# A chunked scan whose operands are laid out by head of a pair in DRAM, with a tied store and a reordered output projection

## The chip, the cores and the metric

One core of a Trainium2 chip runs the whole program. The metric is the device time of one execution in microseconds (us). Engines are named as in the profile: PE (TensorE, its weight loads apart as PEld), DVE (VectorE), ACT (ScalarE), POOL (GpSimd) and SP (SyncE), which here only issues DMAs; its queue is called SPq. Every engine and every queue works its instructions off in the order in which they stand there.

## The reference

Two layers over 1024 tokens of width 1024. Layer 0 is a convolution and gating mixer, layer 1 an RWKV-7 time mixing; after each mixer and after each SwiGLU feed-forward part stands `x <- LN(alpha*x + ...)`. The change touches layer 1's time mixing:

```
r, k, v = projections of shifted x;  decay w, gate g, rate a from low-rank projections
kk = normalized k * k_k;  k = k * (1 + (a - 1) * k_a)          # 16 heads of 64
state = state * w + (state @ -kk) * (kk * a) + v * k           # per token, per head
y_t   = state @ r_t
y = group norm(y) * ln_g + ln_b + sum(r * k * r_k) * v;   mix = (y * g) @ w_out
```

## The kernel before, in words

`build` calls the phases in order: `phase_a` (layer 0's mixer), `ffn` 0, `phase_c` (the projections of layer 1), the scan `phase_d`, `phase_e` (the output projection of the scan's y) and `ffn` 1. Large matmuls are written as three products of fp32r halves (`mm3`, L232 to L234), weights arrive through three raw buffers (tag `wraw`, `raw_load`, L177) and are split by ACT and DVE (`load_unit`, L192 and L193).

**Phase C** computes R, K, KN, KA, SW (decay) channel-major and spills each tile of 128 channels x 512 tokens with one DMA (`spill`, L836) into DRAM tensors `[8 chunks of 128 tokens, 128, 8, 128]`, where the third index is the pair of heads. V is computed token-major and spilled by `do_v` with one DMA per 128 tokens x 512 columns (L1044) into a plain `[1024, 1024]` tensor `scr_v`.

**The scan** has 32 units: 16 chunks of 64 tokens by two groups of four head pairs. One unit holds, on 128 partitions, two heads of a pair in the two halves of the partitions, called e = 0 and 1. A unit's inputs come by 13 DMAs: `load` (L1209) issues SW and KN (L1219), K and KA in four half-partition DMAs (L1223) and R (L1225); `load_v` (L1228) issues UV and V by halves (L1235, L1236). Its result y leaves by two half-partition DMAs (`store`, L1446) into `scr_y`, plain `[1024, 1024]`.

The units are software-pipelined by hand. Step i of the main loop emits first `store` of unit i-1, then `load` of unit i+5 and `load_v` of unit i+2, then interleaves generators by the letters of `ORDER` (L77): E is `cumulate` of unit i+4 (it reads SW on DVE at L1242, and ACT follows at L1248), D `decay` of unit i+3, P `scores` of unit i+2, I `inverse` of unit i+1, C the eight parts of `chain` of unit i. The sixth C holds the state update (pS) and the last two C's the group norm and gate of y: after PE and DVE, y passes through a chain of POOL instructions (L1415 to L1431), the last of which is the multiplication by the gate at L1431. A scheduler orders the instructions of each queue by the program's order and its own model of when inputs and buffers are ready; `pace` ties an instruction behind the last matmul in that schedule without a semaphore. Buffers of the scan come from rings (`rings`, L1177): y has two, V three.

**Phase E** works on tiles of 128 tokens, tt = 0 to 7. `get_y(tt)` loads the 128 x 1024 tile of y with one DMA (through a `wraw` buffer) and the residual `xres` (L1518), applies gain and bias to the residual on POOL (`ln_gain`, L355 and L356), and transposes y on PE (L1525). `mmh(tt, n)` makes half n of the output columns, 24 matmuls. `ln(tt)` normalizes (the power on POOL is L272, the normalized tile ACT L279) and transposes the result on PE (L298). Two tiles' first halves run inside the scan's last steps (`early`). After the scan the order is: the four units of `w_out`'s second half are loaded; tiles 2 and 3 are fetched and their first half made; tiles 4 to 7 are fetched in a row; then the second halves of tiles 0 to 3 with their `ln`; then the second halves of tiles 4 to 7; then their first halves with `ln`.

Of the kernel before, what the change touches and what calls it, by code (L numbers as in the profile page):

```python
# [15 lines left out]
F32 = mybir.dt.float32  # L16
# [9 lines left out]
P = 128  # L26
D = 1024
# [44 lines left out]
HP = 4  # L72
# [1 line left out]
AHEAD = 4  # L74
INV = 1

ORDER = "ICIPCEIPDICPIECDICPICICPDICI"  # L77
SCAN_EARLY = 32


# [9 lines left out]
def build(tc, xT, xtok, w_ab, w_abv, w_abo, cols, rows, hrows, sguw, f_in, f_out, w_r, w_k, w_v, w_o,  # L90
          l_w1, l_a1, l_g1, l_w2, l_a2, l_g2, out, dbg=None):
    nc = tc.nc
    c = Ctx()
    c.tc, c.nc = tc, nc
    c.first_loads = None
    with ExitStack() as es:
        setup(c, es, rows, hrows)
        dram = es.enter_context(tc.tile_pool(name="dram", bufs=1, space=DRAM))
        xres = dram.tile([T, D], F32, name="xres")
        scr = {n: dram.tile([8, P, 8, P], F32, name=f"scr_{n}") for n in ("R", "K", "KN", "KA", "SW")}  # L100
        scrv = dram.tile([T, D], F32, name="scr_v")
        scry = dram.tile([T, D], F32, name="scr_y")

        def show(n, tiles):
            if dbg is not None and n in dbg:
                for i, a in enumerate(tiles):
                    nc.sync.dma_start(dbg[n][i * P:(i + 1) * P, :], a)
        res = [dram.tile([T, D], F32, name=f"res{i}") for i in range(2)]
        hscr = dram.tile([NHT, P, T], F32, name="scr_h")
        xc = phase_a(c, xT, xtok, w_ab, w_abv, w_abo, sguw, cols, res[0])  # L110
        def masks():
            c.scan = scan_const(c)
        x1 = ffn(c, 0, xc, f_in, f_out, "mix0", "ffn0", res[0], hscr, fp32_out=True, spill=xres, aside=masks)
        if dbg is not None and "b" in dbg:
            nc.sync.dma_start(dbg["b"], xres)
        scan = phase_d(c, scr, scrv, scry, l_g2)
        phase_c(c, x1, scr, scrv, w_r, w_k, w_v, l_w1, l_a1, l_g1, l_w2, l_a2, scan)
        if dbg is not None and "R" in dbg:
            for n in scr:
                nc.sync.dma_start(dbg[n], scr[n])  # L120
            nc.sync.dma_start(dbg["V"], scrv)
        xc = phase_e(c, scry, xres, w_o, scan, res[1])
        if dbg is not None and "Y" in dbg:
            nc.sync.dma_start(dbg["Y"], scry)
        ffn(c, 1, xc, f_in, f_out, "mix1", "ffn1", res[1], hscr, final=out)


# [26 lines left out]
def tmp(c, name, dtype=F32):  # L154
    return c.pool.tile([P, 512], dtype, name=name, tag="t", bufs=N_T)
# [673 lines left out]
def phase_c(c, x1, scr, scrv, w_r, w_k, w_v, l_w1, l_a1, l_g1, l_w2, l_a2, scan):  # L829
# [2 lines left out]
    ghid = c.ghid = big(c, "ghid")  # L832

    def spill(n, k, h, src):
        dst = scr[n][4 * h:4 * h + 4, :, k, :].rearrange("c p t -> p c t")
        nc.sync.dma_start(dst, src.rearrange("p (c t) -> p c t", c=4))  # L836

    c.omu = c.const.tile([P, 48], F32, name="omu")
    nc.vector.tensor_scalar(c.omu, c.colr("mu", 0, 48), -1.0, 1.0, op0=ALU.mult, op1=ALU.add)
# [195 lines left out]
    def do_v(h, xi, rest=None, turn=None):  # L1035
        for n in range(2):
            units = [load_unit(c, w_v[n, q]) for q in range(4)]
            for t in range(4):
                p = bank(c, "a", "pv")
                proj_tok(c, p, units, xi, t, turn)  # L1040
                v = sp()
                nc.scalar.copy(v, p)
                tt = h * 4 + t
                nc.sync.dma_start(scrv[tt * P:(tt + 1) * P, n * 512:(n + 1) * 512], v)  # L1044
                if rest and n == t == 0:
                    rest()
                step(7 - n * 4 - t)
# [100 lines left out]
def phase_d(c, scr, scrv, scry, l_g2):  # L1148
# [21 lines left out]
    def rings(plan, n, dtype=F32):  # L1170
        pool, at = Ring(c, plan[0][0], n, sum(k for _, k in plan), dtype).bufs, 0
        for name, k in plan:
# [2 lines left out]
            at += k  # L1175
            R1[name] = r
    rings([("ra", INV + 3), ("bk", 2), ("bktm", NA), ("UV", INV + 3), ("AT", 2 * NA)], 2 * W)  # L1177
    rings([("R", 3), ("cl", 2), ("Em", 2), ("rk", 2), ("S", 2 * NG), ("dS", 2), ("u1", 2), ("y", 2),
           ("V", 3), ("gg", 2), ("bo", 2)], W)
    rings([("E", 4)], HP * (CH + 2))  # L1180
    rings([("TT", 2)], HP * P, F32R)
    rings([("zr", 3)], W, F32R)
# [26 lines left out]
    def load(n, ch, g):  # L1209
        u = Ctx()  # L1210
        u.n, u.ch, u.g = n, ch, g
        ks = slice(g * HP, (g + 1) * HP)
        at = slice(ch % 2 * CH, ch % 2 * CH + CH)
        src = lambda nm, r=slice(0, P): scr[nm][ch // 2, r, ks, at]
        u.ld = {}
        t_ = tmp(c, "ld")
        for e, nm in enumerate(("SW", "KN")):
            u.ld[nm] = A4(t_[:, e * W:(e + 1) * W])
            nc.sync.dma_start(u.ld[nm], src(nm))  # L1219
        u.xk = tmp(c, "ld").rearrange("p (k x t) -> p k x t", k=HP, x=2)  # L1220
        for e in range(2):
            for x, nm in ((e, "K"), (1 - e, "KA")):
                nc.sync.dma_start(u.xk[half[e], :, x, :], src(nm, half[e]))  # L1223
        u.ld["R"] = A4(R1["R"]())
        nc.sync.dma_start(u.ld["R"], src("R"))  # L1225
        us[n] = u

    def load_v(u):  # L1228

        src = scrv[u.ch * CH:(u.ch + 1) * CH, u.g * 2 * W:(u.g + 1) * 2 * W].rearrange(  # L1230
            "t (k e j) -> t e k j", k=HP, e=2)
        u.UV = R1["UV"]().rearrange("p (e k j) -> p e k j", e=2, k=HP)
        u.V = A4(R1["V"]())
        for e in range(2):
            nc.sync.dma_start(u.UV[half[e], e], src[:, e])  # L1235
            nc.sync.dma_start(u.V[half[e]], src[:, e])  # L1236

    def cumulate(u):

# [200 lines left out]
            pass  # L1440

    def store(u):
        dst = scry[u.ch * CH:(u.ch + 1) * CH, u.g * 2 * W:(u.g + 1) * 2 * W].rearrange(
            "t (k e j) -> t e k j", k=HP, e=2)
        for e in range(2):
            nc.sync.dma_start(dst[:, e], u.y[half[e]])  # L1446

    def by_half(name):

# [11 lines left out]
    through(decay(us[0]))  # L1461
    for i in range(-INV - 1, len(seq)):
        gens = {}
        if i > 0:
            store(us[i - 1])
        if i + AHEAD + 1 < len(seq):
            load(i + AHEAD + 1, *seq[i + AHEAD + 1])
        if 0 <= i + INV + 1 < len(seq):
            load_v(us[i + INV + 1])
        if i + AHEAD < len(seq):  # L1470
            gens["E"] = cumulate(us[i + AHEAD])
        if i + INV + 2 < len(seq):
            gens["D"] = decay(us[i + INV + 2])
        if i >= 0:
            gens["C"] = chain(us[i], us.get(i + NG))
        if 0 <= i + INV < len(seq):
            gens["I"] = inverse(us[i + INV])
        if i + INV + 1 < len(seq):
            gens["P"] = scores(us[i + INV + 1])
        if i == 0:  # L1480
            g2 = c.pool.tile([P, 1024], F32, name="g2", tag="w", bufs=N_W)
            nc.sync.dma_start(g2, l_g2)
            g2 = g2.rearrange("p (g k e j) -> p g e k j", g=NG, k=HP, e=2)
            lg, lb = by_half("rln_g"), by_half("rln_b")
        for s in ORDER:
            if s in gens:
                fresh[0] = True
                next(gens[s], None)
                if s in "CIP":
                    yield  # L1490
        for gen in gens.values():
            assert next(gen, "end") == "end"
    store(us[len(seq) - 1])

# [1 line left out]
def phase_e(c, scry, xres, w_o, scan, res):  # L1498
# [12 lines left out]
        return r  # L1511

    def get_y(tt, b):
        y = raw_load(c, scry[tt * P:(tt + 1) * P, :])
        yh = big(c, "yh", F32R).rearrange("p (k t) -> p k t", k=KT)
        yl = big(c, "yl", F32R).rearrange("p (k t) -> p k t", k=KT)
        acc[tt] = big(c, "acc")
        nc.sync.dma_start(acc[tt], xres[tt * P:(tt + 1) * P, :])  # L1518
        ln_gain(c, acc[tt], rows_)
        st[tt] = norm_stats(c, D)  # L1520
        for q in range(2):
            pt = bank(c, b, "pt", [P, 4, P])
            for j in range(4):
                k = q * 4 + j
                c.last_mm = nc.tensor.transpose(pt[:, j, :], y[:, k * P:(k + 1) * P], c.ident)  # L1525
            split(c, yh[:, q * 4:q * 4 + 4, :], yl[:, q * 4:q * 4 + 4, :], pt)
            yield
        ys[tt] = yh, yl
# [39 lines left out]
    assert next(scan, "end") == "end"  # L1568
    through(first)
    units[0][3] = load_unit(c, w_o[0, 3])  # L1570
    units[1] = [load_unit(c, w_o[1, q], arena=True) for q in range(4)]
    done = E_EARLY
    for h in range(2):
        for tt in range(4 * h, 4 * h + 4):
            if ys[tt] is None:
                through(get_y(tt, "b"))
            if tt >= done:
                through(mmh(tt, h, "a"))
        if h == 0:
            for tt in range(4, 8):  # L1580
                through(get_y(tt, "b"))
        for tt in range(4 * h, 4 * h + 4):
            through(mmh(tt, 1 - h, "a"))
            if tt % 4 >= E_LN:
                ln(tt - E_LN)
        for tt in range(4 * h + 4 - E_LN, 4 * h + 4):
            ln(tt)
    return xc


# [77 lines left out]
```

## Time and profile before

| what | value |
|---|---|
| median of 3 runs | 2655.47 us (2653.22 to 2659.98) |
| the profiled execution's own time | 2657.45 us |
| its span | 2655.7 us |
| mean granted PE clock | 0.971 of full |
| PE / PEld / DVE / ACT / POOL busy | 95% / 75% / 64% / 43% / 19% |
| first and last store of the scan's y | 1411.2 and 1858.5 us from the span's start |

A span is cut by the profile into 40 equal slices of 66.4 us. A busy PE is not PE at its peak, since matmuls overlap; idle time is shown with what ended it ("<-"). A wait is put down to the instruction that came last.

### The profile page before, as it was taken

To read this page: it belongs to the slowest core of one execution; us is meant where nothing else is said; L and a number is where in the kernel's file an instruction comes from. 1 tells how busy PE (TensorE), PEld (TensorE's weight loads), DVE (VectorE), ACT (ScalarE), POOL (GpSimd) and SP (SyncE) were. 2 spreads that over 40 slices of the span, in tenths; PEclk is the share of its full clock that TensorE was granted. 3 is DMA by queue.
4 is the path that set the end of the run, shared out by engine and by line. 5 is a ranking of instruction groups with operands and counts; after the bars stand their busy time and mean duration, and the time that the engine had idled before them with its cause. 6 is when DMAs were issued, how large, how long until landed. Compare 5 with 4: busy or idle time off the path is not lost.

```text
span 2655.7 us, 41419 instructions
## 1 busy us (share of the span) xinstructions
PE 2517.7 (95%) x16064; PEld 2004.7 (75%) x16064; DVE 1697.4 (64%) x2981; ACT 1136.5 (43%) x2192; POOL 517.8 (19%) x526
## 2 busy tenths in 40 slices
PE   8999999999999999999998878788899999999997
PEld 6677868888878786777777767676677888878785
DVE  7775596666648428777846667675477666657534
ACT  3115552323323327777746666674352333322230
POOL 0012250000007000010214555465300000006003
PEclk9999999999999999999998789899899999999999
DMA  3403322222235433555764333322223222225451
GB/s 145 125 20 109 115 84 88 87 80 80 81 126 198 150 124 107 163 157 165 207 164 101 91 89 86 76 52 96 105 88 103 80 87 74 86 99 188 146 169 64
DMA packets 257605, 295.79 MB, mean 111 GB/s; under 512 B 149888, under 2 KB 190976, under 8 KB 257408
## 3 DMA queue, kind: packets, MB, share of 16 engines
q1 hardware_dynamic: 256256, 291.05, 35.3%
q8 instruction: 126, 2.06, 0.3%
q10 hardware_dynamic: 1152, 2.10, 0.2%
q14 instruction: 71, 0.58, 0.1%
HBM read 219.56 MB, written 69.21 MB: 109 GB/s over the span
## 4 chain that ended last, share of the span: by engine, by line
PE 65%; DVE 9%; issue 9%; DMA 7%; POOL 6%; ACT 4%; SPq 1%; DVEq 0%; ACTq 0%; POOLq 0%
PE py L646 14%; PE pz L646 9%; PE px L646 8%; DMA wraw<-in_f_out_dram 2%; PE pv L232 2%; PE pd L232 1%; PE pd L233 1%; PE pd L234 1%; PE po L232 1%; PE po L233 1%; PE po L234 1%; PE pv L233 1%; POOL acc L355 1%; PE pv L234 1%; PE pA L1204 1%
## 5 line engine op out<-in xcount | busy, mean ns | idle before, releaser
L646 PE MATMUL py<-xch,wb 128*128 128x512 f32 x1056 | 356.5, 400 | 2.9 <-DVE u L695 2.1
L200 ACT CAST wb<-wraw 128x512 fp32r<-128x512 f32 x220 | 135.6, 619 | 398.6 <-PE py L646 177.4
L232 PE MATMUL pd<-wb,hh 128*128 128x512 f32 x704 | 277.5, 394 | 5.1 <-DVE acc L735 5.0
L234 PE MATMUL pd<-wb,hl 128*128 128x512 f32 x704 | 278.0, 395 | 0.0
L233 PE MATMUL pd<-wb,hh 128*128 128x512 f32 x704 | 277.7, 394 | 0.0
L646 PEld LDWEIGHTS py<-xch,wb 128*128 128x128 f32 x1056 | 199.7, 189 | 61.4 <-DVE u L695 15.3
L203 DVE TENSOR_TENSOR wb<-wraw,wb 128x512 fp32r<-128x512 f32 x220 | 171.8, 784 | 112.9 <-ACT wb L200 110.6
L355 POOL TENSOR_TENSOR acc<-acc,g_row 128x1024 f32<-128x1024 f32 x24 | 65.8, 2743 | 897.6 <-DMA acc<-res 880.3
L646 PE MATMUL px<-xch,wb 128*128 128x512 f32 x704 | 234.4, 396 | 3.3 <-ACT p L657 3.3
L646 PE MATMUL pz<-xch,wb 128*128 128x512 f32 x704 | 233.1, 392 | 4.5 <-ACT xch L200 4.5
L200 ACT CAST wb<-sums 128x512 fp32r<-128x512 f32 x176 | 108.8, 622 | 256.7 <-PE pz L646 145.2
L646 PE MATMUL py<-xcl,wb 128*128 128x512 f32 x528 | 209.0, 396 | 1.6 <-DVE xcl L203 1.6
L203 DVE TENSOR_TENSOR wb<-sums,wb 128x512 fp32r<-128x512 f32 x176 | 123.0, 702 | 102.6 <-ACT wb L200 101.7
L203 DVE TENSOR_TENSOR hl<-wraw,hh 128x1024 fp32r<-128x1024 f32 x72 | 126.9, 1771 | 89.5 <-ACT hh L200 89.4
L1204 PEld LDWEIGHTS <-lt 128*128 128x128 f16 x1792 | 88.0, 102 | 103.2 <-issue 77.7
L232 PEld LDWEIGHTS pd<-wb,hh 128*128 128x128 f32 x704 | 133.1, 189 | 37.3 <-issue 4.4
L646 PEld LDWEIGHTS px<-xch,wb 128*128 128x128 f32 x704 | 132.7, 189 | 35.2 <-ACT p L657 5.5
L646 PEld LDWEIGHTS pz<-xch,wb 128*128 128x128 f32 x704 | 132.0, 188 | 35.0 <-ACT xch L200 5.3
L1204 PE MATMUL pX<-lt 128*128 128x64 f16 x1280 | 92.2, 201 | 69.2 <-DVE lt L1337 38.8
L233 PEld LDWEIGHTS pd<-wb,hh 128*128 128x128 f32 x704 | 132.7, 189 | 30.0
L234 PEld LDWEIGHTS pd<-wb,hl 128*128 128x128 f32 x704 | 132.7, 189 | 29.7
L193 DVE TENSOR_TENSOR wlo<-wraw,whi 128x1024 fp32r<-128x1024 f32 x82 | 103.0, 1262 | 69.9 <-ACT whi L192 46.8
(313 smaller groups left out, 5706.6 us busy)
## 6 DMA issues: line engine op xcount, KB each, us to landing
wraw<-in_f_in_dram SPq DMA_DIRECT2D x96, 512.0 KB, 3.6
wraw<-scr_h SPq DMA_DIRECT2D x72, 512.0 KB, 3.9
scr_h<-hf SPq DMA_DIRECT2D x44, 512.0 KB, 2.6
wraw<-in_f_out_dram SPq DMA_DIRECT2D x88, 256.0 KB, 2.7
res<-acc SPq DMA_DIRECT2D x16, 512.0 KB, 2.6
acc<-res SPq DMA_DIRECT2D x16, 512.0 KB, 4.2
wraw<-in_w_r_dram SPq DMA_DIRECT2D x16, 512.0 KB, 4.0
wraw<-in_w_k_dram SPq DMA_DIRECT2D x16, 512.0 KB, 4.2
```

The lines of the kernel that those rows point to most:

```text
L193: (lo_eng or nc.vector).tensor_tensor(lo, raw, f(hi), op=ALU.subtract)
L200: nc.scalar.copy(hi, src)
L203: return (eng or nc.vector).tensor_tensor(lo, src, f(hi), op=ALU.subtract)
L232: nc.tensor.matmul(ps, ls(ah), rs(bh), start=start, stop=False)
L233: nc.tensor.matmul(ps, ls(ah), rs(bl), start=False, stop=False)
L234: c.last_mm = nc.tensor.matmul(ps, ls(al), rs(bh), start=False, stop=stop)
L355: c.nc.gpsimd.tensor_tensor(x, x, rows[0], op=ALU.mult)
L646: c.last_mm = nc.tensor.matmul(ps, a_[:, k * P:(k + 1) * P], b_[:, k % 2, :], start=start and k == i == 0, stop=False, skip_group_check=True)
L1204: keep(nc.tensor.matmul(*a, **k))
```

## The change

The DRAM tensors get layouts by head: K and KA together as `KB` with the two places that the scan's tile wants side by side, V and y as `[16 chunks, 2 (e), 64 tokens, 8 pairs, 64]`. A unit is loaded by 7 DMAs (SW, KN, KB, R, UV twice, V) and stored by one. The spills of K and KA in phase C take two DMAs each for one, those of V four for one; `get_y` takes four DMAs for one. `store` becomes a generator at a new letter Y in `ORDER`, behind the fifth C of the following step, tied by `pace` behind the last matmul there. The y ring grows from two to three buffers, V's from three to four; the number of arena tiles stays. In phase E tiles 2 and 3 are fetched and multiplied first, with the second half's weights loaded between; then second halves of tiles 0 to 3 with `get_y` of tiles 4 to 7 and `ln` between them; then first halves of tiles 4 to 7, then their second halves with `ln`.

```diff
-ORDER = "ICIPCEIPDICPIECDICPICICPDICI"
+ORDER = "ICIPCEIPDICPIECDICPIYCICPDICI"
...
-        scr = {n: dram.tile([8, P, 8, P], F32, name=f"scr_{n}") for n in ("R", "K", "KN", "KA", "SW")}
-        scrv = dram.tile([T, D], F32, name="scr_v")
-        scry = dram.tile([T, D], F32, name="scr_y")
+        scr = {n: dram.tile([8, P, 8, w, P], F32, name=f"scr_{n}") for n, w in (("R", 1), ("SW", 1), ("KN", 1), ("KB", 2))}
+        scrv, scry = [dram.tile([T // CH, 2, CH, 8, 64], F32, name=f"scr_{n}") for n in "vy"]
...
     def spill(n, k, h, src):
-        dst = scr[n][4 * h:4 * h + 4, :, k, :].rearrange("c p t -> p c t")
-        nc.sync.dma_start(dst, src.rearrange("p (c t) -> p c t", c=4))
+        name, places = dict(K=("KB", (0, 1)), KA=("KB", (1, 0))).get(n, (n, (0,)))
+        m = P // len(places)
+        for e, x in enumerate(places):
+            r = slice(e * m, (e + 1) * m)
+            dst = scr[name][4 * h:4 * h + 4, r, k, x, :].rearrange("c p t -> p c t")
+            nc.sync.dma_start(dst, src[r].rearrange("p (c t) -> p c t", c=4))
...
-                nc.sync.dma_start(scrv[tt * P:(tt + 1) * P, n * 512:(n + 1) * 512], v)
+                v5 = v.rearrange("p (k e j) -> p e k j", k=4, e=2)
+                for i in range(4):
+                    r = slice(i // 2 * CH, i // 2 * CH + CH)
+                    nc.sync.dma_start(scrv[2 * tt + i // 2, i % 2, :, n * 4:n * 4 + 4, :], v5[r, i % 2])
...
-    rings([("R", 3), ("cl", 2), ("Em", 2), ("rk", 2), ("S", 2 * NG), ("dS", 2), ("u1", 2), ("y", 2),
-           ("V", 3), ("gg", 2), ("bo", 2)], W)
+    rings([("R", 3), ("cl", 2), ("Em", 2), ("rk", 2), ("S", 2 * NG), ("dS", 2), ("u1", 2), ("y", 3),
+           ("V", 4), ("gg", 2), ("bo", 2)], W)
...
-        for e in range(2):
-            for x, nm in ((e, "K"), (1 - e, "KA")):
-                nc.sync.dma_start(u.xk[half[e], :, x, :], src(nm, half[e]))
...
+        nc.sync.dma_start(xk.rearrange("p (k t) -> p k t", t=CH), src("KB"))
...
         for e in range(2):
-            nc.sync.dma_start(u.UV[half[e], e], src[:, e])
-            nc.sync.dma_start(u.V[half[e]], src[:, e])
+            nc.sync.dma_start(u.UV[half[e], e], scrv[u.ch, e, :, ks, :])
+        nc.sync.dma_start(u.V, scrv[u.ch].rearrange("e t k j -> (e t) k j")[:, ks, :])
...
     def store(u):
-        dst = scry[u.ch * CH:(u.ch + 1) * CH, u.g * 2 * W:(u.g + 1) * 2 * W].rearrange(
-            "t (k e j) -> t e k j", k=HP, e=2)
-        for e in range(2):
-            nc.sync.dma_start(dst[:, e], u.y[half[e]])
+        dst = scry[u.ch].rearrange("e t k j -> (e t) k j")[:, u.g * HP:(u.g + 1) * HP, :]
+        pace(c, nc.sync.dma_start(dst, u.y))
+        yield
...
-        if i > 0:
-            store(us[i - 1])
...
+        if i > 0:
+            gens["Y"] = store(us[i - 1])
...
     def get_y(tt, b):
-        y = raw_load(c, scry[tt * P:(tt + 1) * P, :])
+        y = c.pool.tile([P, 1024], F32, name="wraw", tag="wraw", bufs=N_RAW)
+        for i in range(2):
+            for e in range(2):
+                nc.sync.dma_start(y[i * CH:(i + 1) * CH].rearrange("t (k e j) -> t e k j", e=2, j=64)[:, e],
+                                  scry[2 * tt + i, e])
...
-    units[1] = [load_unit(c, w_o[1, q], arena=True) for q in range(4)]
-    done = E_EARLY
+    for tt in range(E_EARLY, 4):
+        through(get_y(tt, "b"))
+        through(mmh(tt, 0, "a"))
+        for q in range(2 * tt - 4, 2 * tt - 2):
+            units[1].append(load_unit(c, w_o[1, q], arena=True))
     for h in range(2):
         for tt in range(4 * h, 4 * h + 4):
-            if ys[tt] is None:
-                through(get_y(tt, "b"))
-            if tt >= done:
-                through(mmh(tt, h, "a"))
-        if h == 0:
-            for tt in range(4, 8):
-                through(get_y(tt, "b"))
-        for tt in range(4 * h, 4 * h + 4):
-            through(mmh(tt, 1 - h, "a"))
+            through(mmh(tt, 1, "a"))
+            if h == 0:
+                through(get_y(tt + 4, "b"))
             if tt % 4 >= E_LN:
                 ln(tt - E_LN)
         for tt in range(4 * h + 4 - E_LN, 4 * h + 4):
             ln(tt)
+        if h == 0:
+            for tt in range(4, 8):
+                through(mmh(tt, 0, "a"))
```

## Rows read from the trace of the kernel before

**Rows 1.** The page: span, PE's total, and its busy tenths in 40 slices.

```profile
span 2655.7 us, 41419 instructions
PE 2517.7 (95%) x16064; PEld 2004.7 (75%) x16064; DVE 1697.4 (64%) x2981; ACT 1136.5 (43%) x2192; POOL 517.8 (19%) x526
...
PE   8999999999999999999998878788899999999997
```

**Rows 2.** Timeline of SP: stores of y that begin and end 23 steps.

```profile
1425.65 1.26 SPq L1446 DMA_DIRECT2D scr_y<-R  x2
...
1744.58 1.25 SPq L1446 DMA_DIRECT2D scr_y<-R  x2
```

**Rows 3.** Windows by step: us, each engine's busy time, PEclk, DMA share, GB/s.

```profile
1480.86:1496.27 15.41, 13.37 (x204) 11.42 (x204) 10.49 (x31) 9.98 (x28) 8.31 (x11) 0.78 0.41 101
...
1542.62:1560.74 18.12, 15.82 (x295) 13.38 (x296) 14.57 (x46) 13.48 (x39) 12.84 (x13) 1.00 0.34 82
...
1614.81:1626.91 12.10, 10.28 (x201) 8.86 (x201) 9.88 (x30) 8.85 (x28) 7.51 (x11) 1.00 0.39 88
...
1683.08:1699.05 15.97, 11.42 (x157) 9.41 (x158) 7.80 (x26) 8.00 (x25) 7.38 (x11) 0.75 0.34 75
```

**Rows 4.** Waits from 1405 to 1860: us in total, times, longest.

```profile
ACT E L1248 <- DVE R L1242: 42.8, 20, 4.5
...
DVE R L1242 <- DMA ld<-scr_SW: 29.3, 14, 4.0
```

**Rows 5.** Timeline of the step from 1683.08: start, us, instruction, idle before.

```profile
1683.08 1.25 SPq L1446 DMA_DIRECT2D scr_y<-R  x2
...
1686.11 0.37 SPq L1219 DMA_DIRECT2D ld<-scr_SW  x1
...
1690.05 0.69 DVE L1242 TENSOR_TENSOR_SCAN R<-rst,ld 128x256 f32<-128x256 f32 x1 [4.01 <-DMA ld<-scr_SW]
...
1691.44 0.37 PE L1204 MATMUL pX<-lt 128*128 128x64 f16 x4 [4.03 <-DVE lt L1337]
```

**Rows 6.** Waits of SP's own queue, from 1405 to 1860.

```profile
SPq L1446 <- POOL R L1423: 144.2, 28, 11.1
SPq L1446 <- POOL R L1431: 36.9, 4, 13.7
```

**Rows 7.** DMA issues by tile: ns of one, min/median/max, first and last start.

```profile
L1219 SPq DMA_DIRECT2D ld<-scr_KN x32: 425/506/648, 1309.1 to 1734.2; - x32
...
L1223 SPq DMA_DIRECT2D ld<-scr_K x64: 573/604/1408, 1311.2 to 1738.3; - x64
...
L1235 SPq DMA_DIRECT2D ra<-scr_v x64: 573/574/1464, 1343.3 to 1785.5; - x64
...
L1446 SPq DMA_DIRECT2D scr_y<-R x64: 575/607/1538, 1411.2 to 1858.5; - x64
...
L1044 SPq DMA_DIRECT2D scr_v<-sp x16: 320/332/547, 1174.7 to 1400.9; - x16
```

**Rows 8.** Timelines of 1425 to 1622: pS after a store; a short SW wait.

```profile
1427.94 0.94 PE L1204 MATMUL pS<-ra 128*64 128x64 f32 x16
...
1621.79 0.69 DVE L1242 TENSOR_TENSOR_SCAN R<-rst,ld 128x256 f32<-128x256 f32 x1 [1.08 <-DMA ld<-scr_SW]
```

**Rows 9.** Timeline of PE and POOL in phase E.

```profile
1867.37 1.06 PE L1525 MATMUL pt<-ident,wraw 128*128 128x128 f32 x8 [2.22 <-DMA wraw<-scr_y]
...
1883.79 0.56 POOL L272 TENSOR_TENSOR rstd<-ve,mhalf 128x1 f32<-128x1 f32 x1
...
1886.61 1.97 PE L298 MATMUL pt<-ident,acc 128*128 128x128 f32 x8 [7.81 <-ACT acc L279]
```

**Rows 10.** The window of phase E around the longest of these waits (columns as rows 3).

```profile
1880.00:1890.00 10.00, 3.40 (x12) 3.09 (x13) 3.34 (x9) 3.12 (x5) 4.42 (x4) 0.61 0.13 52
```

**Rows 11.** Timeline of ACT and PE in the scan's last steps.

```profile
1830.44 1.04 ACT L192 CAST whi<-wraw 128x1024 fp32r<-128x1024 f32 x1 [9.79 <-DMA wraw<-in_w_o_dram]
...
1832.08 0.37 PE L1204 MATMUL pX<-lt 128*128 128x64 f16 x4 [6.16 <-ACT lt L1328]
```

**Rows 12.** The page's DMA issues: KB each, median us to landing.

```profile
wraw<-scr_y SPq DMA_DIRECT2D x8, 512.0 KB, 4.3
```

More of the change, by code (lines that the diff above doesn't have):

```diff
@@ L117, in build @@
         phase_c(c, x1, scr, scrv, w_r, w_k, w_v, l_w1, l_a1, l_g1, l_w2, l_a2, scan)
[L118 to L121, printed above, removed]
         xc = phase_e(c, scry, xres, w_o, scan, res[1])
-        if dbg is not None and "Y" in dbg:
-            nc.sync.dma_start(dbg["Y"], scry)
         ffn(c, 1, xc, f_in, f_out, "mix1", "ffn1", res[1], hscr, final=out)
@@ L1213, in load @@
         at = slice(ch % 2 * CH, ch % 2 * CH + CH)
-        src = lambda nm, r=slice(0, P): scr[nm][ch // 2, r, ks, at]
-        u.ld = {}
+        src = lambda nm: scr[nm][ch // 2, :, ks, :, at].rearrange("p k x t -> p (k x) t")
         t_ = tmp(c, "ld")
[L1217 to L1220, printed above, removed]
-        for e in range(2):
-            for x, nm in ((e, "K"), (1 - e, "KA")):
-                nc.sync.dma_start(u.xk[half[e], :, x, :], src(nm, half[e]))
-        u.ld["R"] = A4(R1["R"]())
+        u.ld = dict(SW=A4(t_[:, 0:W]), KN=A4(t_[:, W:]), R=A4(R1["R"]()))
+        xk = tmp(c, "ld")
+        u.xk = xk.rearrange("p (k x t) -> p k x t", k=HP, x=2)
+        nc.sync.dma_start(u.ld["SW"], src("SW"))
+        nc.sync.dma_start(u.ld["KN"], src("KN"))
+        nc.sync.dma_start(xk.rearrange("p (k t) -> p k t", t=CH), src("KB"))
         nc.sync.dma_start(u.ld["R"], src("R"))
@@ L1228, in load_v @@
     def load_v(u):
-        src = scrv[u.ch * CH:(u.ch + 1) * CH, u.g * 2 * W:(u.g + 1) * 2 * W].rearrange(
-            "t (k e j) -> t e k j", k=HP, e=2)
+        ks = slice(u.g * HP, (u.g + 1) * HP)
         u.UV = R1["UV"]().rearrange("p (e k j) -> p e k j", e=2, k=HP)
@@ L1442, in store @@
     def store(u):
-        dst = scry[u.ch * CH:(u.ch + 1) * CH, u.g * 2 * W:(u.g + 1) * 2 * W].rearrange(
-            "t (k e j) -> t e k j", k=HP, e=2)
-        for e in range(2):
-            nc.sync.dma_start(dst[:, e], u.y[half[e]])
+        dst = scry[u.ch].rearrange("e t k j -> (e t) k j")[:, u.g * HP:(u.g + 1) * HP, :]
+        pace(c, nc.sync.dma_start(dst, u.y))
+        yield
     def by_half(name):
@@ L1492, in phase_d @@
             assert next(gen, "end") == "end"
-    store(us[len(seq) - 1])
+    through(store(us[len(seq) - 1]))
 def phase_e(c, scry, xres, w_o, scan, res):
```

## The prediction

> **What bounds the kernel now.** I read the page first. PE is busy 95% of the span, and in nearly every slice of 66.4 us it stands at 9 tenths or more; the one long stretch below that is slices 22 to 28, and those are the scan [rows 1]. So time can be won only there, and where PE waits in the stages right behind it; anything the change adds to phase C lies beside a full PE.
>
> Next I read the scan step by step, from store of y to store of y. Between the two stores shown lie 23 steps and 318.9 us [rows 2], 13.87 us a step. The windows show how unequal they are: one takes 12.10 us with PE busy 10.28, the step at 1683 takes 15.97 with PE busy only 11.42 and the granted clock at 0.75 where the short one had 1.00 [rows 3]. I take 12.10 as a clean step. Twenty-three of these are 278.3 us, so the stretch holds 40.6 us of excess.
>
> The waits say where it comes from. DVE's cumulated sum (L1242) waits 14 times, 29.3 us in all, for the load of SW, and ACT then waits for that sum [rows 4]. The timeline of the slow step shows the whole path: the store of y goes out at 1683.08, the load of SW behind it only at 1686.11, DVE resumes at 1690.05 after 4.01 us of idling, and PE's inverse has idled 4.03 us for DVE when it resumes at 1691.44 [rows 5]. The waits of SP's own queue name what held the load back: the two store DMAs wait 144.2 and 36.9 us for POOL, 181.1 us over 32 units, or 5.7 us a step [rows 6]. The profile puts most of that down to L1423, which starts as the gate multiplication L1431 ends; what the store needs is y from L1431. While it waits, every load for later units queues behind it.
>
> SP has little slack to make up for it. By the medians for KN, K, UV and y [rows 7], pricing SW and R like KN, KA like K and V like UV, one unit's queue costs 3 x 0.506 + 4 x 0.604 + 4 x 0.574 + 2 x 0.607 = 7.4 us of issuing. With 5.7 us of waiting that is 13.1 of 13.87 us: the SP queue is a closed loop with the chain that ends in y.
>
> **The change, part by part.** Fewer DMAs: SW, KN, R and V at 0.506, KB at 0.604 (the costliest load shown; its neighbour KN would give 0.506), UV twice at 0.574, y once at 0.607 make 4.4 us instead of 7.4. These 3.0 us are off the path by themselves: a shorter queue saves time only through loads that come earlier.
>
> The tied store is what moves those. At present it heads a step's DMAs, before y is there. Behind the fifth C it stands just ahead of the pS products, and in the step shown these start at 1427.94, 2.3 us after the store had been released at 1425.65 [rows 2, 8]. So y should be ready when the queue comes to it, and SW, KN, KB, R, UV and V pass ahead. What queues behind the waiting store is then the next step's SW, which has the rest of the step as lead. The third y buffer lets POOL write while an older store is outstanding, and the fourth V buffer keeps V's load from waiting for L1423; I cost both at nothing, since they only keep that queue moving.
>
> What this is worth: of the 40.6 us, one step holds a residual's gain on POOL (18.12 - 12.10 = 6.0), and three hold a weight unit of the output projection; the one shown costs 15.41 - 12.10 less its SW wait of about 1.7, so 1.6 each and 4.9 together [rows 3]. Both stay. That leaves 29.7 us, against 29.3 of SW waits counted directly [rows 4]. Two of these 14, like the 1.08 us at 1621.79 [rows 8], stand in steps that took about 12.1 all the same, so I take 27 and keep 13 to 30 as ends: 13 if another wait fills half the hole, 30 if all goes. What is late next in a clean step is DVE waiting for PE's scores, which is inside the 12.10.
>
> Phase C: V's 16 spills go from 0.332 to four half-partition DMAs, which I price like y's halves: 16 x (4 x 0.607 - 0.332) = 33.5 us more issuing. The 32 spills of K and KA go to two each: 32 x (2 x 0.607 - 0.332) = 28.2. All 61.7 us lie on SP beside a PE that is full in these slices (16 to 20) [rows 1]; the three raw buffers cover weights that queue behind a spill. I take +1, with 0 and 61.7 as ends; a gain is excluded, as nothing there gets shorter.
>
> Phase E: now the residual gains of tiles 4 to 7 run on POOL in one row, and the first normalization's power (L272) queues behind them until 1883.79; PE's transposes wait 7.81 us for it, until 1886.61. Just before, PE waits 2.22 us for a tile of y [rows 9]. The window around the long wait has PE busy 3.40 us at a granted 0.61, a mix of its levels of 1.2 and 2.4 GHz [rows 10]; at the upper level throughout that would be at most 1.7 us less. In the new order a 24-matmul half lies between two gains, so the power waits for one tile's gain at most, and the last tiles of y are asked for long after their stores. I take 9 of these 11.7 us. The second half's weights are now loaded between tiles 2 and 3: four units that could be late instead; hence 0 as the other end.
>
> In the scan's last steps ACT waits 9.79 us for a weight whose load had queued behind a store, and PE 6.16 us for ACT [rows 11]. The tied store and later weights make this less likely, but POOL's gains still run there: I take 2, ends 0 and 6.
>
> Four DMAs for a tile of y cost 4 x 0.607 us of issuing in pieces of 256 bytes. Windows show such pieces cost engine time: the clean step moves 88 GB/s at a DMA share of 0.39, or 226 at full share, while 1880 to 1890 with long rows moves 52 at 0.13, or 400 [rows 3, 10]. For 512 KB that is 2.3 us against 1.3. A tile landed in 4.3 us before [rows 12], so about 5.3 plus issue, requested one 24-matmul half ahead: nothing on the path.
>
> The Trainium skill (DMA: Bandwidth & Descriptors, Specifications) speaks against this part: it says that transfers under 512 bytes fall below line rate because they are handled as read-modify-write. The two windows agree in direction, 226 against 400 GB/s; by the rule alone the rearranged V spills and y tiles would be a loss, while V's and y's scan-side runs, now 1 KB, would be a gain of the same kind.
>
> **Sum.** 27 + 9 + 2 - 1 = 37 us off the profiled execution's own 2657.45 us gives 2620.5. That execution is 2.0 us above the median of 2655.47, within its runs.
>
> **The rivals.** (a) The scan gains, phase E does not: the second half's weights, now fetched behind tiles of y and behind the last stores, hold PE where POOL did. For it speaks the 9.79 us wait of exactly this kind [rows 11]; against it that three raw buffers work ahead. Time 2657.45 - 27 + 1 = 2631.5. Chance 0.20.
>
> (b) Half the scan's gain goes to a new wait: y is late on POOL also at its new place, the store blocks SP half a step later, and the next SW is late again. For it: 181 us of store waits [rows 6] are a lot to bring to nothing. Against: 2.3 us of room in the step shown [rows 2, 8]. Time 2657.45 - 13 + 1 = 2645.5. Chance 0.10.
>
> (c) The loads are hidden already. Then SW's lateness is only a symptom of a slow chain, and the step is set by PE, DVE and POOL; time 2657, no change. For it: units are loaded about a step ahead. Against: DVE idles 4.01 us on the load with PE behind it [rows 5]. Chance 0.05.
>
> The Trainium skill has the rule for (c) (DMA: Bandwidth & Descriptors, Rules for kernel authors): issue a DMA early and wait late, and its fixed setup cost overlaps with compute. By that rule fewer DMAs bring nothing; the 14 waits [rows 4] disagree, as issuing early is what the queue prevents.
>
> (d) Slower: phase C's spills fill SP's queue, weight loads come late behind them, and PE waits. The price fully exposed is 61.7 us, and with the other gains kept the time is 2657.45 + 61.7 - 38 = 2681. It decides once spills delay a weight by more than the two spare raw buffers hold. Against: V's 16 spills start between 1174.7 and 1400.9 [rows 7], so their 33.5 us of issuing are spread over more than 200. Chance 0.04. My forecast keeps 0.61.
>
> **The numbers.** The low end takes 30 + 11.7 + 6 us and a clean step up to 0.3 us shorter without its own SW wait (23 x 0.3 = 7): 2603. The high end, 2646, takes in (a) and the middle of (b). Outside lie (c), (d), the worse half of (b) and some 5% below: about 0.19. A change of 0.3%, 8 us, is what a measurement of this kernel can tell. Faster: 0.61 + 0.20 + 0.08 of (b) = 0.89; same: (c) and the rest of (b), 0.07; slower: (d), 0.04.
>
> **What would show it.** Right: DVE's waits for SW gone or under 5 us; store waits of SP under 60 us from 181; steps near 12.1 but for the gain and weight steps, with the clock at 1.00 in most; no PE wait over 3 us on the first normalization. Wrong: SW waits as before with a store ahead of each; PE waits on weights in phase C, or in phase E on the second half's; steps that stay near 13.9 while SP idles.

## The result and the profile after

The kernel after takes 2611.14 us (median of 4 runs, 2608.92 to 2611.84) beside 2654.34 us (4 runs) of the kernel before: a ratio of 0.9832, interval 0.9817 to 0.9847. The forecast was 2620.5 in 2603 to 2646. The profiled execution took 2611.84 us with a span of 2610.1. Of all the runs below one, the 2889.98 us of the kernel with the tie and four V buffers, was in a slow state of the chip, and its ratio leaves it out. The page of after, beside [rows 1]:

```profile
span 2610.1 us, 41343 instructions
PE 2490.9 (95%) x16064; PEld 1984.1 (76%) x16064; DVE 1715.3 (66%) x2981; ACT 1137.8 (44%) x2192; POOL 518.2 (20%) x526
...
PE   8999989999999999999998888889999999999997
...
PEclk9999999999999999999999989999999999999998
```

PE does the same 16064 matmuls in 27 us less busy time. Most of that is in the scan, over the 22 steps between the two stores of [rows 2] and the same steps of after (windows of before and of after, columns as [rows 3]):

```profile
1425.65:1744.58 318.93, 264.23 (x4494) 225.97 (x4495) 218.14 (x643) 204.24 (x599) 170.82 (x223) 0.87 0.37 86
...
1426.47:1716.50 290.03, 246.87 (x4510) 211.30 (x4509) 229.01 (x644) 204.47 (x599) 173.40 (x223) 0.94 0.36 91
```

PE idles 43.2 us there instead of 54.7, and its products take 17.4 us less, at a granted clock of 0.94 instead of 0.87.

Two rows cut a profile into stages: the scan is from the first to the last pA product (products of the scan's scores), the output projection from there to the last po product (those with the output weights). Before, by tile (ns of one, min/median/max, first and last start):

```profile
L1204 PE MATMUL pA<-ra x512: 272/272/579, 1341.0 to 1802.2; 64*128 64x128 f32 x171
...
L234 PE MATMUL po<-whi,yl x124: 388/395/628, 1812.3 to 1950.9; 128*128 128x512 f32 x124
```

After, the same view:

```profile
L1207 PE MATMUL pA<-ra x512: 271/272/374, 1342.1 to 1771.8; 64*128 64x128 f32 x171
...
L230 PE MATMUL po<-whi,yl x124: 388/393/629, 1781.8 to 1906.9; 128*128 128x512 f32 x124
```

| stage | before | after | gain | forecast |
|---|---|---|---|---|
| up to the scan | 1341.0 | 1342.1 | -1.1 | -1 |
| scan | 461.2 | 429.7 | 31.5 | 27 |
| output projection, with the scan's tail | 148.7 | 135.1 | 13.6 | 9 + 2 |
| rest | 704.8 | 703.2 | 1.6 | 0 |

The stages are those of one profiled execution each, and add up to 45.6 us; the medians of all runs differ by 43.2.

Now the scan. The windows of after (columns as [rows 3]):

```profile
1426.47:1445.28 18.81, 15.69 (x214) 13.43 (x211) 17.48 (x35) 10.54 (x30) 13.66 (x12) 0.68 0.45 126
1614.55:1627.33 12.78, 10.51 (x207) 8.93 (x207) 10.13 (x30) 9.19 (x28) 7.46 (x10) 1.00 0.33 83
```

The second is the ordinary step: between 1576 and 1704 ten steps in a row take 12.78 to 12.84 us, and in the one shown the granted clock is 1.00. The first holds the residual's gain, which in before stood in the step of 18.12 us. Waits of after, from 1405 to 1860 (us in total, times, longest), beside [rows 4]:

```profile
ACT E L1247 <- DVE R L1241: 17.6, 22, 1.2
...
DVE R L1241 <- DMA ld<-scr_SW: 14.9, 17, 1.2
```

and those of SP's queue, beside [rows 6]:

```profile
SPq L1235 <- POOL R L1422: 111.9, 25, 7.9
...
SPq L1443 <- POOL R L1430: 38.4, 6, 11.4
```

The long waits for SW are gone, short ones stay. The store no longer waits in most steps (38.4 us from 181.1), but the load of V (L1235) now does, for the same end of y on POOL: 111.9 us. So the wait for POOL has not left SP's queue, it has changed its owner; yet the scan is 31.5 us shorter. The experiments ask why.

### The profile page after: what moved, and what is told of

Read it like the earlier page. It is cut to its first block, busy times and chain, and to the rows that moved or that the text cites. A ratio compares the mean times of both kernels' runs of the same rounds, so it can differ in the third digit from the quotient of the medians.

```text
span 2610.1 us, 41343 instructions
## 1 busy us (share of the span) xinstructions
PE 2490.9 (95%) x16064; PEld 1984.1 (76%) x16064; DVE 1715.3 (66%) x2981; ACT 1137.8 (44%) x2192; POOL 518.2 (20%) x526
## 5 line engine op out<-in xcount | busy, mean ns | idle before, releaser
L268 POOL TENSOR_TENSOR rstd<-ve,mhalf 128x1 f32<-128x1 f32 x48 | 36.1, 754 | 520.4 <-DVE ve L266 484.8
```

What stands on the lines that cost most here:

```text
L268: c.last_pow = nc.gpsimd.tensor_tensor(r, ve, c.mhalf[:, 0:1], op=ALU.pow)
```

## The experiments

A ratio is to the kernel before, run on the same chip. Its medians there lie between 2649.7 and 2654.9 us, so kernels that are less than 5 us apart are compared by their ratios. Scan and stage times are those of one profiled execution of each kernel.

### Which part makes the scan shorter

**Layouts alone.** The kernel after with the store untied at the step's head, the old rings and the old output projection:

```diff
-ORDER = "ICIPCEIPDICPIECDICPIYCICPDICI"
+ORDER = "ICIPCEIPDICPIECDICPICICPDICI"
-... ("y", 3), ("V", 4)
+... ("y", 2), ("V", 3)
-        pace(c, nc.sync.dma_start(dst, u.y))
+        nc.sync.dma_start(dst, u.y)
...
```

> The changed kernel with the new DRAM layouts and merged DMAs alone: the store stands untied at the head of a step again, y has two buffers and V three, phase E has its old order. Theory (the scan's gain comes from the store leaving the head of SP's queue; the number of DMAs matters little, as SP idles in the time that a wait takes from it): the store still waits over 100 us in all for y, DVE still waits 15 to 30 us for SW, and the time is 2640 to 2656 us. Rival (3 us less issuing a unit is what brings the loads forward): SW waits under 5 us, steps near 12.8, and 2622 to 2630 us, that is all of the scan's gain of some 31 us without phase E's 13.

2621.33 us, 0.9886 (0.9861 to 0.9911); the scan takes 430.6 us, as good as after. SP's waits, from 1380 to 1860:

```profile
SPq L1443 <- POOL R L1430: 158.4, 32, 11.5
```

SP's timeline in an ordinary step:

```profile
1618.39 0.37 SPq L1222 DMA_DIRECT2D ld<-scr_SW  x1
1618.80 0.93 SPq L1223 DMA_DIRECT2D ld<-scr_KN  x1
1623.02 0.33 SPq L1443 DMA_DIRECT2D scr_y<-R  x1
1623.59 0.33 SPq L1235 DMA_DIRECT2D R<-scr_v  x1
```

The store waits nearly as long as before, but SW's load stands ahead of it, issued 4.6 us earlier. In the step of before that [rows 5] shows, it stood behind: first came the store, then V's load, then SW's.

```profile
1684.44 1.25 SPq L1236 DMA_DIRECT2D R<-scr_v  x2
```

But that was not so in every step of before. Of the 23 loads of SW that it issues between 1411 and 1760, 14 go out directly behind V's load, and DVE's sum then waits at 13 of them. Eight go out some 5 us or more ahead of V's load, and the sum waits at none, as at the next one after the step of [rows 5]:

```profile
1695.31 0.36 SPq L1219 DMA_DIRECT2D ld<-scr_SW  x1
...
1702.74 1.21 DVE L1242 TENSOR_TENSOR_SCAN R<-rst,ld 128x256 f32<-128x256 f32 x1
```

The theory had the waits right (158.4 us of the store, 23.9 for SW from 1340 to 1870) and the time wrong; the rival had the time within 1 us and the waits wrong.

**Tie alone.** The kernel before with Y in `ORDER`, the two store DMAs behind `pace`, and three y buffers:

```diff
-ORDER = "ICIPCEIPDICPIECDICPICICPDICI"
+ORDER = "ICIPCEIPDICPIECDICPIYCICPDICI"
-            nc.sync.dma_start(dst[:, e], u.y[half[e]])
+            pace(c, nc.sync.dma_start(dst[:, e], u.y[half[e]]))
...
```

> The kernel before with the store tied behind the fifth C, as two half-partition DMAs, and the third y buffer; layouts, 13 loads a unit, V's three buffers and phase E as before. Theory (the place of the store is the cause): store waits fall from 181 us to under 60, steps come down to about 13, and the time is 2622 to 2632 us. Rival (DMA count): with 7.4 us of issuing a unit left and loads that wait for their buffers in the same queue, SW waits stay at 20 to 30 us and the time at 2645 to 2658 us.

2667.50 us, 1.0056 (1.0037 to 1.0075): slower. SP's waits from 1340 to 1870:

```profile
SPq L1236 <- POOL R L1423: 140.2, 27, 8.5
...
SPq L1446 <- POOL R L1423: 17.7, 2, 11.1
SPq L1446 <- POOL R L1431: 3.3, 1, 3.3
```

SP's timeline in one step:

```profile
1624.45 1.23 SPq L1236 DMA_DIRECT2D R<-scr_v  x2
1625.79 0.55 SPq L1219 DMA_DIRECT2D ld<-scr_SW  x1
```

and the waits of the other engines, from 1340 to 1870:

```profile
DVE R L1242 <- DMA ld<-scr_SW: 33.5, 17, 3.8
```

The tie did what it says: the store's waits fell from 181.1 us to 21.0. But V's load waits in its place, SW still stands behind the waiting DMA, and DVE waits for it as before (33.5 for 29.3 us). Both theories fall; the rival had the waits nearly right, but neither range reaches 2667.50. (The text on record speaks of 13 loads; they are 11, with two stores.)

**One part less.** After with V's ring at three, and after untied but with all its rings and the new output projection:

```diff
-           ("V", 4), ...
+           ("V", 3), ...
```

> The changed kernel with V's ring at three buffers for four, nothing else. In the changed kernel V's load waits 112 us in SP's queue for the multiplication that frees its buffer (L1422). Theory (a load that waits in SP's queue holds the loads behind it, so an earlier-freed buffer is worth time): V's wait grows, SW comes later, and the time is 2618 to 2640 us. Rival (SP has room for that wait, since what binds is the freeing of the load buffers by DVE): 2608 to 2614 us, within 0.15% of the changed kernel.

2614.79 us, 0.9862 (0.9841 to 0.9884), between the two ranges; scan 433.7 us, 4.0 more than after. V's load waits 131.8 us, but SW's stands ahead of it.

```diff
-        pace(c, nc.sync.dma_start(dst, u.y))
+        nc.sync.dma_start(dst, u.y)
...
```

> The changed kernel with only the store untied: it stands at the head of a step again, as one DMA; layouts, three y and four V buffers and phase E's new order stay. Theory (the tie is worth most of the scan's 31 us): store waits come back to over 100 us and the time is 2630 to 2642 us. Rival (with fewer DMAs and the fourth V buffer the place of the store no longer matters): 2609 to 2616 us.

2613.84 us, 0.9857 (0.9841 to 0.9874); scan 433.9 us. The store's waits came back (149.2 us), but not the time: the rival was right. With the layouts in place the tie and the fourth buffer are worth some 4 us of the scan each, at the edge of what these intervals tell from nothing.

### It is the order in SP's queue

**Tie and four V buffers, old layouts**: the tie alone, and one number:

```diff
-           ("V", 3), ...
+           ("V", 4), ...
```

> The kernel before (old layouts, 11 loads and 2 stores a unit, old phase E) with the tied store and three y buffers as in e2, and V's ring at four for three. Nothing else differs from e2, but in SP's queue the load of SW now stands ahead of V's load, which waits for POOL, and no longer behind it. Theory (what counts is whether SW stands ahead of or behind the one DMA that waits for POOL): the scan falls by 25 us or more and the time is 2618 to 2632 us, with as many DMAs as before. Rival (DMA count or row length in DRAM is what counts): 2645 to 2668 us.

2609.10 us, 0.9836 (0.9814 to 0.9859): all 13 DMAs a unit, and as fast as after. SP's timeline:

```profile
1616.07 0.55 SPq L1219 DMA_DIRECT2D ld<-scr_SW  x1
1616.67 0.51 SPq L1219 DMA_DIRECT2D ld<-scr_KN  x1
1619.50 1.25 SPq L1236 DMA_DIRECT2D R<-scr_v  x2
1620.79 1.27 SPq L1446 DMA_DIRECT2D scr_y<-R  x2
```

In this schedule V's load comes later, and SW goes out 3.4 us ahead of it instead of 1.3 us behind it. V's load still waits 68.2 us in all, but no wait of DVE for SW is left, and the scan takes 420.9 us, less than in after. The time is below even the theory's range.

**After with SW pushed behind V's load.** The reverse test: `load_v` is emitted first, and `after` (the order-only tie under `pace`) puts SW behind it:

```diff
+        if behind is not None:
+            after(c, d, behind)      # d: the DMA of SW, behind: that of V
...
```

> The changed kernel with one change of order: the load of SW is tied behind the load of V of the same step, which waits for POOL; layouts, 8 DMAs, rings and the tied store stay. Theory (queue order): SW waits grow to 25 us or more, the short DMAs notwithstanding, and the time is 2630 to 2660 us. Rival (8 DMAs leave SP room enough): 2609 to 2618 us.

2672.44 us, 1.0082 (1.0059 to 1.0105); scan 493.6 us. SP's timeline:

```profile
1635.22 0.33 SPq L1237 DMA_DIRECT2D R<-scr_v  x1
1635.61 0.43 SPq L1222 DMA_DIRECT2D ld<-scr_SW  x1
```

The waits of the other engines, from 1340 to 1870:

```profile
DVE R L1243 <- DMA ld<-scr_SW: 61.6, 23, 3.8
```

Eight DMAs a unit, the tied store, the fourth buffer and the new output projection are all there, and the kernel is slower than before, 61 us above after and above the theory's range. With `load_v` emitted first, the other loads move a little in the queue too, but SW's is the only DMA that an engine waits for between 1405 and 1760.

**More DMAs at the same place.** After with KB loaded by four half-partition DMAs and V by two, so that a unit is again loaded by 11:

```diff
-        nc.sync.dma_start(xk.rearrange("p (k t) -> p k t", t=CH), src("KB"))
+        for e in range(2):
+            for x in (0, 1):
+                nc.sync.dma_start(u.xk[half[e], :, x, :], scr["KB"][ch // 2, half[e], ks, x, at])
...
```

> The changed kernel with the loads of KB and V cut up again: KB in four and V in two half-partition DMAs, from the new layouts, so 11 loads a unit for 7; the tied store and all else stay. Theory (SP has slack; issuing alone is not on the path): the 4 x 0.6 = 2.4 us of issuing a unit are hidden, 2609 to 2617 us. Rival (DMA count is what binds): half or more of the scan's 31 us is lost, 2627 to 2645 us.

2614.71 us, 0.9855 (0.9838 to 0.9871): 3.6 us above after by the medians, which the intervals don't tell from nothing. The theory was right. The Trainium skill (DMA: Bandwidth & Descriptors, Rules for kernel authors) says to use one transfer over all partitions in place of two over disjoint halves, and to coalesce small ones; no run here shows a gain from that by itself.

All 14 kernels together. "Behind" counts the loads of SW, of those issued between 1411 and 1760, that go out directly behind V's load or the store; the waits are DVE's for SW in the same stretch:

| kernel | DMAs a unit | SW's loads behind | waits for SW, us | scan, us |
|---|---|---|---|---|
| before | 13 | 14 of 23 | 29.3 | 461.2 |
| new output projection alone | 13 | 14 of 23 | 26.4 | 459.8 |
| tie alone | 13 | 22 of 23 | 32.3 | 480.2 |
| after, SW pushed behind V | 8 | 22 of 22 | 57.7 | 493.6 |
| after / old output projection | 8 | 0 / 0 of 22 | 14.9 / 16.8 | 429.7 / 430.0 |
| layouts alone | 8 | 0 of 22 | 20.2 | 430.6 |
| untied / V ring 3 | 8 | 2 of 23 / 1 of 22 | 21.9 / 20.4 | 433.9 / 433.7 |
| after, halves | 12 | 6 of 24 | 4.1 | 436.1 |
| tie and V ring 4 / with new output projection | 13 | 4 / 4 of 23 | 0 / 0 | 420.9 / 422.2 |
| after, ninth buffer (below) | 8 | 20 of 22 | 16.3 | 422.5 |
| after, sum paced (below) | 8 | 18 of 23 | 0 | 456.2 |

In the first twelve kernels, those with SW mostly behind take 459.8 us or more and those with SW mostly ahead 436.1 or less, and the number of DMAs sorts nothing. The last two do not fit: with the ninth buffer SW goes out behind the store, which follows V's load, and the scan is short all the same; with the sum paced no wait for SW is left, so that its place in the queue can't be what makes that scan long. And the waits for SW are not the whole price: they fall by 14.4 us from before to after, where the scan falls by 31.5, and they don't sort the kernels with SW ahead.

### What still holds a step at 12.78 us

In after DVE's sum still waits 0.7 us in an ordinary step. The timeline, all engines:

```profile
1606.62 0.43 DVE L1270 TENSOR_TENSOR ra<-ld,E 128x256 f32<-128x256 f32 x1 [0.37 <-PE pz L1207]
...
1609.27 1.08 DVE L1241 TENSOR_TENSOR_SCAN R<-rst,ld 128x256 f32<-128x256 f32 x1 [0.71 <-DMA ld<-scr_SW]
```

and SP's:

```profile
1607.07 0.36 SPq L1222 DMA_DIRECT2D ld<-scr_SW  x1
```

The decay L1270 ends at 1607.05 and frees the buffer (eight buffers, two a unit: one for SW and KN, one for K and KA); SW's load goes out at once, and the sum that needs it stands 2.65 us behind the decay, closer than the load takes (2.5 us from issue to landing by the median). Two tries, a ninth buffer and a later sum:

```diff
-N_ARENA, N_W, N_RAW, N_T = 34, 9, 3, 8
+N_ARENA, N_W, N_RAW, N_T = 34, 9, 3, 9
```

> The changed kernel with nine buffers of the tag t for eight, so that the load of SW takes a buffer that was freed earlier. In the changed kernel SW is issued the moment DVE's L1270 frees its buffer and the cumulated sum stands a few instructions behind it, so each of 17 steps waits 0.7 to 1.2 us. Theory (that wait is what keeps a step at 12.78 where steps without loads take 11.8): SW waits under 3 us in all, steps 12.0 to 12.4, and 2597 to 2605 us. Rival (the wait is slack that PE or POOL would need anyway): steps stay at 12.7 to 12.9 and the time at 2608 to 2614 us.

2598.74 us, 0.98 (0.9786 to 0.9815): 12 us below after by the medians and some 8 by the ratios, 7.2 us of it in the scan. But the waits for SW remain (20.4 us from 1340 to 1870, in after 22.0), and SW moved in the queue too, to right behind the store:

```profile
1618.78 0.34 SPq L1235 DMA_DIRECT2D R<-scr_v  x1
...
1620.93 0.50 SPq L1443 DMA_DIRECT2D scr_y<-R  x1
1621.53 0.38 SPq L1222 DMA_DIRECT2D ld<-scr_SW  x1
```

So the time is as the theory had it, its reason is not shown, and a load of SW behind V's does not make a step long in every kernel.

```diff
-        nc.vector.tensor_tensor_scan(flat(cl), ...)
+        ins = nc.vector.tensor_tensor_scan(flat(cl), ...)
+        if n > 4:
+            pace(c, ins)
```

> The changed kernel with DVE's cumulated sum (L1241) tied behind the last matmul of its place in the program, so that the scheduler no longer moves it up to right behind the instruction that frees the buffer of its load. Theory: SW waits under 3 us in all, as the load has a step of lead; if the later place costs nothing else, 2597 to 2606 us. Rival: the sum now stands so close ahead of its own unit's decay that DVE waits for ACT's exponentials in its place, and the time is 2610 to 2640 us.

2636.81 us, 0.9939 (0.9925 to 0.9954): no wait for SW is left, and it is slower than after, within the rival's range. An ordinary step takes 13.64 us, and SW's load fell behind V's, so the run does not price the sum's place alone; it shows that an engine's wait may go and the time rise.

### The output projection

**After with the old order there**:

```diff
-    for tt in range(E_EARLY, 4):
-        through(get_y(tt, "b"))
...
+    units[1] = [load_unit(c, w_o[1, q], arena=True) for q in range(4)]
...
```

> The changed kernel with phase E in its old order (four weight units first, tiles 4 to 7 fetched in a row, their second half before their first); the scan is the changed one. Theory (phase E's order gives some 13 us of its own, by taking the power of the first normalization out from behind four residual gains): 2620 to 2627 us, with PE again waiting 5 to 8 us for the first normalized tile. Rival (the time behind the scan fell because the tied store lets the last weights come earlier): 2611 to 2615 us.

2608.54 us, 0.9836 (0.9817 to 0.9854); the stage takes 134.4 us, in after 135.1. Beside the other parts the new order brings nothing. The rival expected that, at 2611 to 2615 us; its reason was not tried.

**Before with the new order alone** (the same block the other way):

```diff
-    units[1] = [load_unit(c, w_o[1, q], arena=True) for q in range(4)]
...
+    for tt in range(E_EARLY, 4):
+        through(get_y(tt, "b"))
...
```

> The kernel before with phase E's new order alone (tiles of y still fetched by one DMA). If the order is worth what the forecast gave it, the 7.8 us wait for the first normalized tile goes and the time is 2641 to 2648 us; if it is worth nothing because the tie or the layouts bring the same, as e3 showed with them in place, 2651 to 2658 us.

2633.74 us, 0.9935 (0.9915 to 0.9955), below the range of either expectation. The stage falls from 148.7 to 125.6 us, by 23.1, and PE has no wait over 1 us in it. The median falls by 16.0 us on the same chip, and the interval allows 12 to 23; so the order alone is worth some 12 to 23, and after shows 13.6 for it and all the rest.

**Tie, four V buffers and the new order, old layouts**: the kernel of 2609.10 with that block.

> The kernel before with old layouts and 13 DMAs a unit, plus the tied store, three y and four V buffers (as e9) and phase E's new order with one DMA for a tile of y (as e11): the whole change without its layouts. Theory (queue order gives the scan's gain, phase E's order the rest, and cutting a tile of y into four DMAs takes part of it back in the changed kernel): the scan from first to last product of scores is 418 to 424 us as in e9, the stretch from there to the last product of the output projection 124 to 130 us as in e11, and the time is 2588 to 2598 us, below the changed kernel. Rival (both gains come out of the same stretch, as e3 suggested): 2604 to 2612 us.

2594.97 us (5 runs), 0.977 (0.9757 to 0.9783): 16 us below after, clear of its interval and in the theory's range. It is after without the layouts. Beside the tie and the four V buffers the order brings 14.1 us of the stage, which takes 140.2 us in the kernel of 2609.10. The scan takes 422.2 us (after 429.7), the output projection 126.1 (135.1).

Where the layouts lose those 9 us is read from the stretch between the last store of y and the last po product. In after it is 90.45 us, with PE busy 83.92 at a clock of 0.96 (windows, columns as [rows 3]):

```profile
1816.45:1906.90 90.45, 83.92 (x390) 68.32 (x389) 57.25 (x104) 33.83 (x58) 27.81 (x17) 0.96 0.50 141
```

In the kernel without the layouts it is 79.80, with PE busy 79.54:

```profile
1810.90:1890.70 79.80, 79.54 (x385) 65.08 (x385) 55.55 (x102) 32.46 (x57) 28.57 (x17) 1.00 0.42 147
```

Of the 10.65 us, 6.3 are idle time of PE (90.45 - 83.92 against 79.80 - 79.54) and 4.4 slower products. The idle time is mostly three waits of PE for the split of y (2.54, 1.95 and 1.28 us), each behind the same pattern. The first, in the timeline of after:

```profile
1836.16 0.56 POOL L268 TENSOR_TENSOR rstd<-ve,mhalf 128x1 f32<-128x1 f32 x1 [2.04 <-DVE ve L266]
1836.68 2.35 POOL L351 TENSOR_TENSOR acc<-acc,g_row 128x1024 f32<-128x1024 f32 x1
1836.75 2.30 DVE L272 SCALAR_TENSOR_TENSOR nb<-bmv,rstd 128x1 f32<-128x1 f32 x1 [0.67 <-POOL rstd L268]
1838.97 1.27 DVE L199 TENSOR_TENSOR yl<-pt,yh 128x512 fp32r<-128x512 f32 x2
...
1839.70 1.11 PE L294 MATMUL pt<-ident,acc 128*128 128x128 f32 x4 [2.54 <-DVE yl L199]
```

POOL ends the normalization's power and starts a residual's gain at once; DVE's next instruction, one element wide, starts 0.07 us after the gain and ends with it, at 2.30 us instead of 0.16; the split of y queues behind it on DVE, and PE waits for the split. (At the other two ACT comes between: its normalization waits for the same instruction, and its half of the split stands behind that.) That instruction's line in after (ns of one, min/median/max):

```profile
L272 DVE SCALAR_TENSOR_TENSOR nb<-bmv,rstd x7: 159/161/2334, 1834.2 to 1905.7; 128x1 f32<-128x1 f32 x7
```

and in the kernel without the layouts:

```profile
L276 DVE SCALAR_TENSOR_TENSOR nb<-bmv,rstd x8: 158/159/160, 1824.1 to 1894.4; 128x1 f32<-128x1 f32 x8
```

There, where a gain follows a power, it waits for the residual's load and starts later, so nothing is held. The long form (2.33 to 2.35 us at its longest) is in all nine kernels with the layouts and in none of the five without, where the longest is 0.16. That goes with the layouts; which of their DMAs moves the gain was not tried, so the four DMAs of a y tile are a suspect and no more.

## Why the prediction was right, and where it was not

**The chain was right.** A DMA that waits at the head of SP's queue holds SW's load, DVE's sum and then PE: pushing SW's load behind the wait costs 64 us of scan, letting it ahead gives 30 and more. The ninth buffer is the exception that limits this. Also right: fewer DMAs "are off the path by themselves"; the phase C term, 1 for 1.1 us, although the spills cost what was priced (0.607 and 0.614 us each); rivals (c) and (d) did not happen.

**"The tied store is what moves those" failed.** The tie alone is slower by 0.56%, with the store's waits gone. The step looked at the wait of one DMA and did not ask which other DMA waits for the same instruction of POOL: V's load. What decides in twelve of the fourteen kernels is whether SW stands ahead of that wait or behind it. The layouts put it ahead with or without the tie; the tie does so only with the fourth V buffer. So that the tie is in the change is not why the scan fell: untied, it takes 433.9 us.

**"I cost both at nothing" failed.** That is the fourth V buffer in the old layouts: the tie without it has 2667.50 us, with it 2609.10. The third y buffer was not tried alone.

**Rival (b), a wait in the old one's place, came half true.** It came: 111.9 us on V's load. It cost little, because SW is ahead of it.

**The scan's 27 came out near 31.5 on a wrong count.** Between the two stores of [rows 2] lie 23 stores, but 22 steps; by line, on POOL between them, one L1431 a step:

```profile
L1431 POOL TENSOR_TENSOR R<-R 128x256 f32<-128x256 f32 x22 | 16.1, 730 | 1.7
```

So a step took 318.9 / 22 = 14.50 us, not 13.87, and the excess over 12.10 was 52.7 us, not 40.6. The agreement of "29.7 us, against 29.3 of SW waits" was an accident of that slip; rightly counted, 52.7 - 6.0 - 4.9 = 41.8, and SW's waits were 29.3 of it. In after the same 22 steps take 290.0 us, 28.9 less. That this is near SW's 29.3 is luck again: the waits for SW only fell to 14.9, by 14.4, and shorter products at the higher clock make 17.4 of the 28.9. The sum took the waits for SW for the whole price and let nearly all of them go; half of them went, and the lower clock of the waiting steps was not in it. The clean step stayed at 12.78 and not "near 12.1". "DVE's waits for SW gone or under 5 us" was wrong too. The store's waits, at 38.4 us, are under the 60 said, and no wait of PE on the first normalization is over 3 us.

**The output projection's 9 + 2 met 13.6 by two errors.** The order alone takes 23.1 us off the stage (16 off the median), since 7.81 + 2.22 + 6.16 us of PE waits [rows 9, 11] go and products at a lower clock with them, which the step had held to 1.7. And the change took about 9 back through POOL's gain beside DVE. The forecast said of the power that it "waits for one tile's gain at most"; what waits is the DVE instruction behind the power. Rival (a) is refuted by the order alone.

**In front of the prediction** it says that a unit's inputs come by 13 DMAs. They are 11, and two stores make 13; the prediction's sum of 7.4 us counted these 13. Against a step of 14.50 us, SP's 13.1 us leave 1.4 us of slack, where the prediction's 13.87 left 0.8.

**Open** are four things: why the scheduler puts SW where it does in each kernel (only the order is shown); why the tie alone is slower than before, at nearly the same waits for SW; why the ninth buffer's scan is short with SW behind; and what makes a clean step 12.47 us with the old layouts and 12.78 with the new.

## What to carry to other kernels

In a queue that works in order, look for every DMA that waits for the late engine, not only for the longest waiter, and read which loads stand behind it; here a tie, a layout and a buffer changed the time mostly by changing that order, so compare the issue order of both kernels before pricing DMAs. Run each part of a change alone and in pairs: here the change without its layouts beat the whole by 16 us. And count intervals, not events.

## What the runs showed of the hardware that was not expected

A DVE instruction one element wide (128x1) took 2.30 to 2.33 us in place of 0.16 where a POOL multiplication over 128x1024 had started just before it, and ended with it. The Trainium skill (SBUF — State Buffer, SBUF: two separate sides) has the rule: a DVE instruction with two SBUF inputs and a POOL instruction that reads SBUF lock each other out for a whole instruction. The trace agrees: three of after's instructions at L272 are held, and each starts less than 0.1 us after the gain and ends with it.

The time to landing grew far less than the size: by the medians of the DMA issues in the trace 64 KB of K took 2.8 us and 128 KB of SW 2.6 before, and 256 KB of KB 3.7 after.
